# Seven block products in place of eight for the values of stage two of an attention layer

## The chip, the cores and the metric

The kernel runs on one core of a Trainium2 chip. The core has TensorE for matmuls (it accumulates into eight banks of PSUM, 128 partitions of 512 float32 each), VectorE, ScalarE and GpSimd for the rest, and SyncE (SP), whose queue issues most of the transfers between DRAM and SBUF. The program gives each engine its instructions in the order in which it emits them; semaphores order the engines among each other. The metric is device time in microseconds (us) for one execution; lower is better.

## The reference

One layer: RMS norm, one input projection into q, k, v and a gate (1024 to 4096 columns), neighbourhood attention over a grid of 32 x 64 tokens with 16 heads of 64, gate, output projection, residual, final RMS norm. Sequence 2048, model width 1024, float32.

```python
def rmsnorm(x, g):
    xf = x.astype(jnp.float32)
    y = xf * lax.rsqrt(jnp.mean(xf * xf, axis=-1, keepdims=True) + RMS_EPS)
    return (y * g.astype(jnp.float32)).astype(x.dtype)

def neighbourhood_mixer(h, w_in, rpb):
    B, S, _ = h.shape
    proj = h @ w_in
    q, k, v, gate = jnp.split(proj, 4, axis=-1)
    heads = lambda a: a.reshape(B, S, N_HEADS, HEAD_DIM)
    o = neighbourhood_attention(heads(q), heads(k), heads(v), rpb)
    return o.reshape(B, S, D_INNER), gate

...
        h = rmsnorm(x, g)
...
            o, gate = neighbourhood_mixer(h, w_in, rpb)
...
        x = x + (o * jax.nn.silu(gate)) @ w_out
    return rmsnorm(x, norm_f)
```

The change concerns `v`, for the second half of the tokens.

## The kernel before

**Precision.** Every float32 matrix is split into a high part h (rounded by a ScalarE copy into float32r) and a low part l = x - h (a VectorE subtraction). A product is three matmuls: h h, h l and l h. One split is therefore one ScalarE and one VectorE operation on a tile of 128 x 512.

**Stages.** Tokens are worked in two halves of 1024, each as two chunks of 512 columns. Stage one (`stage_one`) takes chunks 0 and 1: first the values (two groups u of four head pairs, 512 columns each, token tiles t = 0 to 7 of 128), then twelve *units* of q, k and gate columns. Stage two (`stage_two`) takes chunks 2 and 3: values for token tiles 8 to 15, then nine units. After that the rest of the projections is mixed with attention, and at last comes the output projection.

**Seven products.** The q, k and gate units already use seven block products in place of eight (`seven_products`). The normalised x of a half is cut into blocks Bij (model rows i, chunk j), the weights into Aij (A12: output block 1, model rows 2). `order7` and `uses` say which sum meets which:

```python
order7 = (1, 6, 2, 7, 5, 4, 3)
uses = {1: ("A11", "B11"), 2: ("A12", "B21"), 3: ("S4", "B22"), 4: ("A22", "T4"),
        5: ("S1", "T1"), 6: ("S2", "T2"), 7: ("S3", "T3")}
```

S1 = A21 + A22, S2 = S1 - A11, S3 = A11 - A21 and S4 = A12 - S2 are sums of weights; T1 to T4 are sums of x blocks in the same manner. A product is 12 matmuls of 128 x 128 by 128 x 512 (4 blocks of 128 model rows, 3 matmuls each). P1 gets a bank; a copy of it (`keep`) is kept in SBUF, and P2 adds into the same bank, which then is finished. P6 gets a bank; VectorE writes the bank plus the copy of P1 to u ("2"), then P7 adds into the bank, u ("3") is made, then P4 adds. P5 gets a third bank, and P3 adds into it. So a product that adds into a bank waits for the VectorE or ScalarE operation that reads the bank before it. `run` emits, after each product, what reads its bank, then what is left of the product before (`give`: scale or gate, and a store to DRAM a few matmuls later), then `ahead` (weight loads for unit n + 2, sums for unit n + 1, splits of weights six products ahead), then `also`, with hooks by unit m and product i. In stage one the outputs of chunks 0 and 1 are multiplied by the inverse norm after the product, three of four on GpSimd (line 458); in stage two x is normalised before.

**Values before the change.** In stage two the values are the plain sum over eight blocks: `pair` and `values_of` (line 562) take each of 16 (u, t) tiles with 8 x 3 matmuls, u = 0 in pairs of token tiles, u = 1 mostly one tile at a time. Weights come in raw (`load_v0`) and are split (`split_v`, lines 542 and 545); weights of u = 0 are loaded and, for three of four blocks, split during the last unit of stage one. `evac_v` (line 394) copies a finished bank to SBUF with ScalarE, and a store to `vd` follows. Between the tiles stand, written out by hand, the normalisation of chunk 3 (`normed`, line 516, which needs the spread inverse norm of `spread_rstd(3)`), the splits of x (lines 520 and 521), the sums T (lines 908 to 916) and the first weights of the units (`ahead`).

**Buffers.** `wp` holds eight slots for split weights, `raw` six for raw weights, `xs` 32 for split x blocks, `ev` eight for outputs on their way to DRAM; a pool's slot is reused once all readers of its last tile are done. `store(key, lag, f)` issues f some matmuls later in the order of emission; `due` counts matmuls.

Of the kernel before, what the change touches and what calls it, by code (L numbers as in the profile page):

```python
# [10 lines left out]
F32 = mybir.dt.float32  # L11
# [60 lines left out]
def build(ctx, tc, x, xr, xt, wg, rpb, last, w_out, n0, nf, masks, out):  # L72
    nc = tc.nc
# [4 lines left out]
    sgd = [dram.tile([128, S], F32, name=f"sgd{p}") for p in range(NP)]  # L78
    vd = [dram.tile([4, S, 128], F32, name=f"vd{u}") for u in range(2)]
    ogd = [dram.tile([128, 4, NP, 128], F32, name=f"ogd{T}") for T in range(4)]  # L80
    wod = {f: dram.tile([128, 4, 2, 512], F32, name=f"wod{f}") for f in ("T1", "T2", "T3", "T4")}

    def pool(name, bufs):
# [431 lines left out]
    def normed(f, c, k, t):  # L515
        nc.vector.scalar_tensor_tensor(t, t, gain(f, k), rb[c], op0=OP.mult, op1=OP.mult)
# [56 lines left out]
    def stage_one():  # L573
# [30 lines left out]
            for t, j in hs:  # L604
                square(t, j, rows_in.pop((t, j)))

        def also(n, i):
            m = n + len(us) - 1
            if (m, i) == (4, 0):
                reorder_rstd(0)  # L610
                reorder_rstd(1)
# [189 lines left out]
    def stage_two():  # L801
# [3 lines left out]
        for k in range(4):  # L805
            load_x(2, "x22", k, x22[k])
        slots = {"T2": [(mp, 512)] * 8,
                 "T3": [(sp, 512)] * 2 + sixth[:5] + [(lp, 512)],
                 "T4": [(vh, 512)] * 4 + [(mp, 512)] * 2 + [sixth[5], (qp, 512)]}

        OW = {}

# [61 lines left out]

        ahead, run = seven_products(units_two, 2, X2, also)

        def pair(u, ts, *do):
            for b in range(4):
                values_of(X2, u, ts, (2 * b, 2 * b + 1))
                if b < len(do):  # L880
                    do[b]()

        def both(*fs):
            return lambda: [f() for f in fs]

        def block(f, x, *ks):
            def g():
                if f not in X2:
                    X2[f] = [(xs([128, 512], F32R, "h"), xs([128, 512], F32R, "l")) for _ in range(4)]
                for k in ks:  # L890
                    normed(f, 3, k, x[k])
                    split_to(*X2[f][k], x[k], None)
            return g

        def w(u, b):
            return lambda: [split_v(u, a, b) for a in range(2)]

        def lw(u, *bs):
            return lambda: [load_v0(u, a, b) for b in bs for a in range(2)]

        def v(u, *ts):
            return lambda: [evac_v(u, t, ps[t]) for t in ts]

        def t123(*ks):
            def g():
                for k in ks:
                    a, b, c = x11[k], x12[k], x22[k]
                    nc.vector.tensor_tensor(c, c, b, OP.subtract)
                    nc.vector.tensor_tensor(b, b, a, OP.subtract)
                    nc.vector.tensor_tensor(a, a, c, OP.add)  # L910
            return g

        def t4(*ks):
            def g():
                for k in ks:
                    nc.vector.tensor_tensor(x21[k], x21[k], x11[k], OP.subtract)
            return g

        def form(f, x, *ks):
            def g():  # L920
                for k in ks:
                    h, l = (place_of(a) for a in slots[f][2 * k:2 * k + 2])
                    X2.setdefault(f, []).append((h, l))
                    split_to(h, l, x[k], None)
            return g

        def t1(*ks):
            def g():
                for k in ks:
                    split_to(*X2["B12"][k], x12[k], None)  # L930
                X2["T1"] = X2["B12"]
            return g
# [800 lines left out]
```

## Time and profile before

| | us |
|---|---|
| median of 3 runs | 1047.72 |
| lowest, highest | 1047.21, 1049.62 |
| the profiled execution, device time | 1047.92 |
| its span, first to last instruction | 1046.1 |
| stage one's values end, its units begin | 95.4 |
| stage two's values | 325.3 to 412.9 |
| stage two's units begin | 412.9 |

In the profile PE is TensorE's matmuls, PEld its weight loads, DVE VectorE, ACT ScalarE, POOL GpSimd, SPq the queue of SP. A row of a group reads: line, engine, operation, out<-in by the program's names, shape, count | busy us, mean ns of one | idle time of the engine before them, and what ended it. A timeline row reads: start, length, engine, line, operation, count, and in brackets the idle time before it. Records of matmuls overlap, as the array is pipelined.

### The profile page before, as it was taken

Reading aid. Unit: us, or ns where it says so; the run is one execution under the profiler, and the core shown is the slowest. Engines: PE = TensorE matmul, PEld = TensorE weight load, DVE = VectorE, ACT = ScalarE, POOL = GpSimd, SP = SyncE. Lnnn points to the kernel's source line nnn. Section 1 sums busy time; section 2 is a strip of 40 time slices with the busy share of each in tenths; the row PEclk is TensorE's granted clock in tenths of the full one; section 3 lists DMA queues with packets and bytes.
Section 4 is the critical chain, followed back from the end, with each engine's and each line's share of the span. In section 5 each row is a group of like instructions: output and inputs, shape, how many; then the busy total and the mean of one; then the engine's idle time right before and its main releaser. Section 6 shows DMA issues by size and latency. Waiting matters only on the chain.

```text
span 1046.1 us, 20290 instructions
## 1 busy us (share of the span) xinstructions
PE 1035.6 (99%) x7256; PEld 848.4 (81%) x7256; DVE 736.4 (70%) x1606; ACT 558.0 (53%) x1305; POOL 263.0 (25%) x352
## 2 busy tenths in 40 slices
PE   9999999999999999999999999999999999999997
PEld 6888888887888888888888788888888787888876
DVE  5375657778897724766765775667777788777876
ACT  7545323344344334333434477787888877664433
POOL 0000231221221000000000476765556432420000
PEclk9999999999999999999999999999999999999999
DMA  8733544442736424556565777878777599899553
GB/s 300 243 101 101 141 142 132 131 148 94 211 97 197 121 81 106 206 174 218 179 206 191 231 243 216 251 212 280 252 236 247 182 276 311 270 339 382 134 167 101
DMA packets 133213, 205.30 MB, mean 196 GB/s; under 512 B 12216, under 2 KB 56504, under 8 KB 133112
## 3 DMA queue, kind: packets, MB, share of 16 engines
q1 hardware_dynamic: 131240, 200.99, 61.1%
q0 software_dynamic: 1440, 2.62, 1.7%
q8 instruction: 57, 0.93, 0.4%
q10 hardware_dynamic: 432, 0.40, 0.1%
q14 instruction: 44, 0.36, 0.1%
HBM read 145.24 MB, written 58.72 MB: 195 GB/s over the span
## 4 chain that ended last, share of the span: by engine, by line
PE 95%; DVE 2%; DMA 1%; ACT 1%; issue 0%; SPq 0%; ACTq 0%; DVEq 0%
PE pp L438 37%; PE pv L562 17%; PE py L1463 9%; PE s L1073 8%; PE o L1180 8%; PE ph L1158 4%; PE pp L384 2%; PE pp L386 2%; PE pp L382 2%; PE po L1381 2%; PE po L1383 2%; PE po L1385 2%; DMA sgt<-sgd 1%; DVE f L421 0%; DMA vt<-vd 0%
## 5 line engine op out<-in xcount | busy, mean ns | idle before, releaser
L438 PE MATMUL pp<-h,f 128*128 128x512 f32 x672 | 217.4, 389 | 0.0
L1087 ACT ACTIVATE x<-x,st 128x360 f32<-128x360 f32 (+5 forms) x256 | 151.2, 593 | 24.8 <-DVE st L1081 24.8
L438 PEld LDWEIGHTS pp<-h,f 128*128 128x128 f32 x672 | 126.1, 188 | 26.2
L438 PE MATMUL pp<-t,f 128*128 128x512 f32 x558 | 141.7, 389 | 0.1
L1101 POOL TENSOR_SCALAR x<-x,st 128x480 f32<-128x480 f32 (+5 forms) x192 | 114.5, 614 | 94.3 <-DVE st L1092 92.0
L438 PE MATMUL pp<-l,f 128*128 128x512 f32 x336 | 130.7, 389 | 0.0
L458 POOL TENSOR_TENSOR tmp<-tmp,rb 128x512 f32<-128x512 f32 x36 | 58.4, 1622 | 270.4 <-DVE tmp L456 233.6
L1081 DVE CUSTOM_DVE_ANT_0 x<-s,em 128x360 f32<-128x360 f32 (+5 forms) x256 | 123.0, 535 | 0.6 <-PE s L1073 0.5
L438 PEld LDWEIGHTS pp<-t,f 128*128 128x128 f32 x558 | 104.7, 188 | 22.3 <-DVE u L451 0.6
L1041 POOL TENSOR_TENSOR em<-e,mk 128x264 f32<-128x264 f32 (+3 forms) x64 | 50.8, 824 | 259.5 <-DMA mk<-in_masks_dram 246.0
L421 DVE TENSOR_TENSOR f<-raw,f 128x512 fp32r<-128x512 f32 x105 | 76.5, 728 | 41.8 <-ACT f L420 41.8
L1073 PE MATMUL s<-kt,q 64*128 64x480 f32 (+5 forms) x512 | 95.3, 487 | 0.1
L1180 PEld LDWEIGHTS o<-pta,vt 120*64 120x64 f32 (+2 forms) x1792 | 80.9, 137 | 14.4 <-DVE st L1081 13.6
L562 PE MATMUL pv<-wh,h 128*128 128x512 f32 x256 | 89.1, 394 | 0.7 <-ACT wh L542 0.7
L562 PE MATMUL pv<-wl,h 128*128 128x512 f32 x256 | 88.6, 391 | 0.0
L562 PE MATMUL pv<-wh,l 128*128 128x512 f32 x256 | 88.6, 391 | 0.0
L1180 PE MATMUL o<-pta,vt 120*64 120x128 f32 (+5 forms) x1792 | 85.5, 253 | 0.5 <-DVE pta L1134 0.4
L1073 PEld LDWEIGHTS s<-kt,q 64*128 64x128 f32 x512 | 64.7, 186 | 16.3 <-DVE pta L1134 2.1
L420 ACT ACTIVATE f<-raw 128x512 fp32r<-128x512 f32 x105 | 63.5, 623 | 20.0 <-PE pp L438 8.3
L438 PEld LDWEIGHTS pp<-l,f 128*128 128x128 f32 x336 | 63.1, 188 | 13.1
L1134 DVE COPY pta<-ph 120x512 f32<-120x512 f32 (+5 forms) x96 | 56.9, 639 | 23.7 <-PE ph L1158 23.5
L1134 ACT ACTIVATE pta<-ph 120x512 f32<-120x512 f32 (+5 forms) x96 | 49.7, 557 | 37.0 <-PE ph L1158 36.2
(187 smaller groups left out, 1836.3 us busy)
## 6 DMA issues: line engine op xcount, KB each, us to landing
raw<-in_wg_dram SPq DMA_DIRECT2D x124, 256.0 KB, 4.3
row<-in_xr_dram SPq DMA_DIRECT2D x32, 256.0 KB, 4.8
vd<-v SPq DMA_DIRECT2D x32, 256.0 KB, 2.6
sgd<-sg SPq DMA_DIRECT2D x32, 256.0 KB, 2.9
q<-qd SPq DMA_DIRECT2D x32, 256.0 KB, 5.5
sgt<-sgd SPq DMA_DIRECT2D x32, 256.0 KB, 5.7
ogd<-og SPq DMA_DIRECT2D x32, 256.0 KB, 3.5
kt<-kd SPq DMA_DIRECT2D x16, 480.0 KB, 6.5
```

The source lines that it names most:

```text
L420: nc.scalar.activation(t[:, 0], src, AF.Copy)
L421: nc.vector.tensor_tensor(t[:, 1], src, t[:, 0].bitcast(F32), OP.subtract)
L438: nc.tensor.matmul(B[n, P], t[:, int(m == 2), c], x[k][int(m == 1)], start=P in (1, 6, 5) and k == 0 and m == 0, stop=k == 3 and m == 2, s ...
L458: nc.gpsimd.tensor_tensor(tmp, tmp, rb[c], OP.mult)
L562: nc.tensor.matmul(ps[t], a[:, o], b, start=k == 0 and m == 0, stop=k == NK - 1 and m == 2)
L1073: nc.tensor.matmul(pst[s], qt[a, qs], kt[a, :r1 - r0, c0:c1].rearrange("p r (s c) -> p s r c", c=8), start=True, stop=True)
L1081: nc.vector.tensor_tensor_reduce(X[i, C][s], pst[s], EM[p, ROW_TYPE[T], COL_TYPE[C], s], -1.0, 1e38, OP.add, OP.min, st[:, o:o + 1])
L1087: nc.scalar.activation(X[i, C][s], X[i, C][s], AF.Exp, bias=st[:, o:o + 1], scale=-1.0, accum_out=st[:, 4 + o:5 + o])
L1101: nc.gpsimd.tensor_scalar(X[i, C][s], X[i, C][s], st[:, o:o + 1], 1.0, op0=OP.mult, op1=OP.mult)
L1134: (nc.vector.tensor_copy if h else lambda o, i_: nc.scalar.activation(o, i_, AF.Copy))(t[:k, h, b * 512:b * 512 + w], banks_[b, h][:k, :w])
L1180: nc.tensor.matmul(to.rearrange("d (h q) -> d h q", q=64) if nq > 64 else to, vt[:k, strip, s * 64:s * 64 + 64], t[:k, h, at:at + 64] if n ...
L1463: nc.tensor.matmul(B[m, P], t[:, a, c], b, start=P in (1, 6, 5) and k == 0 and i == 0, stop=k == 3 and i == 2, skip_group_check=True)
```

## The change

Stage two's values become seven products as well. The blocks are the same; now the weights are the moving operand: Aij are blocks of the value weights (A11 and A12: u = 0 with model rows 1 and 2; A21 and A22: u = 1), and each product has four tiles of 128 tokens. A product's tile i is 12 matmuls of one `values_product(P, i)`; the order is P1, P2, P6, P7, P5, P4, P3, four tiles each. U1 (ScalarE, half of P1), U2 and U3 (VectorE) take the places of the copies above. P2's tiles go out through ScalarE as before, the outputs of P5, P4 and P3 through VectorE (`give_v`), which adds U as it scales by 0.5.

The sums S1 to S4 of the value weights are made during stage one's units 0 to 7: in units 0, 2, 4 and 6 (one quarter j of the weights each) four loads at product 0 (`value_rows`) and four VectorE sums at products 3 to 6 (`value_sum`); S1 and S4 are stored raw to `vsd`. In units 1, 3, 5 and 7 S3 and S2 are split (`value_split`, products 1 and 3) and their halves are stored to `vsp`. In stage two `load_s` brings split S2 and S3 straight into `wp` slots, and S1, S4 and A22 raw, to be split by `split_s`. `plan` gives, for each tile, what is emitted behind it. The raw weights of u = 1 are no longer loaded there, except A22. `spread_rstd(3)` moves ahead of the first product; the sums T2 and T3 now go to tiles of their own, so x11 and x22 keep their values for T1, T4 and B22; T1 gets its own tiles instead of overwriting the split B12, which is no longer made. The first `ahead` calls for the units come six to nine tiles (of 12 matmuls) before the end instead of eight to nine tiles of 24. T3 and T4 exchange one slot (`lp`, `qp`).

```diff
@@ -78,6 +78,8 @@
+    vsd = {f: dram.tile([4, 128, 512], F32, name=f"vsd{f}") for f in ("S1", "S4")}
+    vsp = {f: dram.tile([4, 2, 128, 512], F32, name=f"vsp{f}") for f in ("S2", "S3")}
@@ -604,8 +606,40 @@
+        VS = {}
+        def value_rows(j):
+            spot = mkp([128, 3, 512], F32, "vs")
+            homes = [spot[:, k] for k in range(3)] + [kp([128, 960], F32, "vs")[:, :512]]
+            a, b = j % 2, j // 2
+            for f, u, h in (("A21", 1, 0), ("A22", 1, 2), ("A11", 0, 0), ("A12", 0, 2)):
+                VS[f] = homes.pop()
+                o = 512 * (b + h)
+                nc.sync.dma_start(VS[f], wg[KINDS["v"] + 2 * u + a, :, o:o + 512])
+        def value_sum(j, f):
+            a, b, to, o = {"S1": ("A21", "A22", "A22", OP.add), "S3": ("A11", "A21", "A21", OP.subtract),
+                           "S2": ("S1", "A11", "A11", OP.subtract), "S4": ("A12", "S2", "A12", OP.subtract)}[f]
+            nc.vector.tensor_tensor(VS[to], VS[a], VS[b], o)
+            VS[f] = s = VS[to]
+            if f in vsd:
+                store(("vs", f, j), 3, lambda: nc.sync.dma_start(vsd[f][j], s))
+        def value_split(j, f):
+            h, l = ev([128, 512], F32R, "vsh"), ev([128, 512], F32R, "vsl")
+            split_to(h, l, VS[f], None)
+            for i, s in enumerate((h, l)):
+                store(("vs", f, j, i), 5, lambda i=i, s=s: nc.sync.dma_start(vsp[f][j, i], s.bitcast(F32)))
         def also(n, i):
             m = n + len(us) - 1
+            if m < 8:
+                if m % 2 == 0 and i == 0:
+                    value_rows(m // 2)
+                if m % 2 == 0 and i in (3, 4, 5, 6):
+                    value_sum(m // 2, ("S1", "S3", "S2", "S4")[i - 3])
+                if m % 2 == 1 and i in (1, 3):
+                    value_split(m // 2, "S3" if i == 1 else "S2")
@@ -805,8 +839,8 @@
-                 "T3": [(sp, 512)] * 2 + sixth[:5] + [(lp, 512)],
-                 "T4": [(vh, 512)] * 4 + [(mp, 512)] * 2 + [sixth[5], (qp, 512)]}
+                 "T3": [(sp, 512)] * 2 + sixth[:5] + [(qp, 512)],
+                 "T4": [(vh, 512)] * 4 + [(mp, 512)] * 2 + [sixth[5], (lp, 512)]}
@@ -874,77 +908,143 @@
...
-        def w(u, b):
-            return lambda: [split_v(u, a, b) for a in range(2)]
-        def lw(u, *bs):
-            return lambda: [load_v0(u, a, b) for b in bs for a in range(2)]
-        def v(u, *ts):
-            return lambda: [evac_v(u, t, ps[t]) for t in ts]
...
+        U1, U2, U3, B = {}, {}, {}, {}
+        w_of = {1: ((0, 0), (0, 1)), 2: ((0, 2), (0, 3)), 3: (("S4", 0), ("S4", 1)), 4: (("A22", 0), ("A22", 1)),
+                5: (("S1", 0), ("S1", 1)), 6: (("S2", 0), ("S2", 1)), 7: (("S3", 0), ("S3", 1))}
+        def load_s(q, *js):
+            for j in js:
+                if q in vsp:
+                    a, b = j % 2, j // 2
+                    if a == 0:
+                        W[q, b] = wp([128, 2, 512], F32R, "wh"), wp([128, 2, 512], F32R, "wl")
+                    for i, t in enumerate(W[q, b]):
+                        nc.sync.dma_start(t[:, :, a * 256:a * 256 + 256].bitcast(F32), vsp[q][j, i].rearrange("p (k c) -> p k c", c=256))
+                    continue
+                VR[q, j] = t = raw([128, 512], F32, "raw")
+                nc.sync.dma_start(t, wg[KINDS["v"] + 2 + j % 2, :, 1024 + 512 * (j // 2):1536 + 512 * (j // 2)] if q == "A22" else vsd[q][j])
+        def split_s(q, *js):
+            for j in js:
+                a, b = j % 2, j // 2
+                if a == 0:
+                    W[q, b] = wp([128, 2, 512], F32R, "wh"), wp([128, 2, 512], F32R, "wl")
+                h, l = (t[:, :, a * 256:a * 256 + 256] for t in W[q, b])
+                split_to(h, l, VR.pop((q, j)).rearrange("p (k c) -> p k c", c=256), None)
+        def half(to, ps, u):
+            nc.vector.scalar_tensor_tensor(to, ps, 0.5, u, op0=OP.mult, op1=OP.add)
+        def give_v(u, t, ps, add):
+            v = ev([128, 512], F32, "v")
+            half(v, ps, add)
+            dst = vd[u].rearrange("h n d -> n h d")[t * 128:t * 128 + 128]
+            written.add(("v", u, t))
+            store(("v", u, t), 8, lambda: nc.sync.dma_start(dst, v.rearrange("p (h d) -> p h d", h=4)))
+        def values_product(P, i):
+            if P in (1, 6, 5):
+                B[P, i] = bank(512, "pv")
+                for Q in {1: (2,), 6: (7, 4), 5: (3,)}[P]:
+                    B[Q, i] = B[P, i]
+            ps = B[P, i]
+            f = uses[P][1]
+            o = slice(i * 128, i * 128 + 128)
+            for k in range(4):
+                x, w = X2[f][k], [a[:, k % 2] for a in W[w_of[P][k // 2]]]
+                for m, (a, b) in enumerate(((x[0], w[0]), (x[0], w[1]), (x[1], w[0]))):
+                    nc.tensor.matmul(ps, a[:, o], b, start=P in (1, 6, 5) and k == 0 and m == 0, stop=k == 3 and m == 2,
+                                     skip_group_check=True)
+                    due(1)
+            if P == 1:
+                U1[i] = ep([128, 512], F32, "u1") if i < 2 else kp([128, 960], F32, "u1")[:, :512]
+                nc.scalar.activation(U1[i], ps, AF.Copy, scale=0.5)
+            elif P == 2:
+                evac_v(0, 8 + i, ps)
+            elif P == 6:
+                U2[i] = ev([128, 512], F32, "u2")
+                half(U2[i], ps, U1[i])
+            elif P == 7:
+                U3[i] = xp([128, 512], F32, "u3")
+                half(U3[i], ps, U1[i])
+            elif P == 5:
+                give_v(1, 12 + i, ps, U3[i])
+            elif P == 4:
+                give_v(1, 8 + i, ps, U1[i])
+            else:
+                give_v(0, 12 + i, ps, U2[i])
+        T3, T2 = {}, {}
+        def norm(f, x, *ks):
+            for k in ks:
+                normed(f, 3, k, x[k])
+        def sum3(*ks):
+            for k in ks:
+                T3[k] = xs([128, 512], F32, "t3")
+                nc.vector.tensor_tensor(T3[k], x22[k], x12[k], OP.subtract)
+        def sum2(*ks):
+            for k in ks:
+                T2[k] = xs([128, 512], F32, "t2")
+                nc.vector.tensor_tensor(T2[k], x11[k], T3[k], OP.add)
+        def sum1(*ks):
+            for k in ks:
+                nc.vector.tensor_tensor(x12[k], x12[k], x11[k], OP.subtract)
+        def sum4(*ks):
+            for k in ks:
+                nc.vector.tensor_tensor(x21[k], x21[k], T2[k], OP.subtract)
         def form(f, x, *ks):
-            def g():
-                for k in ks:
+            for k in ks:
+                if f in slots:
                     h, l = (place_of(a) for a in slots[f][2 * k:2 * k + 2])
-                    X2.setdefault(f, []).append((h, l))
-                    split_to(h, l, x[k], None)
-            return g
-        def t1(*ks):
-            def g():
-                for k in ks:
-                    split_to(*X2["B12"][k], x12[k], None)
-                X2["T1"] = X2["B12"]
-            return g
-        pair(0, (8, 9), both(w(0, 3), lambda: spread_rstd(3)), both(lw(1, 0), block("B12", x12, 0, 1)), block("B12", x12, 2, 3),
-             block("B22", x22, 0, 1))
-        pair(0, (10, 11), both(v(0, 8, 9), block("B22", x22, 2, 3)), t123(0), t123(1), lw(1, 1))
-        pair(0, (12, 13), v(0, 10, 11), t123(2), t123(3), both(t4(0, 1, 2, 3), lw(1, 2)))
-        pair(0, (14, 15), both(v(0, 12, 13), w(1, 0)), both(w(1, 1), lw(1, 3)), w(1, 2), w(1, 3))
-        pair(1, (12,), v(0, 14, 15), form("T2", x11, 0), form("T2", x11, 1))
-        pair(1, (13,), both(v(1, 12), form("T2", x11, 2)), form("T2", x11, 3))
-        pair(1, (14,), both(v(1, 13), form("T3", x22, 0)), form("T3", x22, 1))
-        pair(1, (15,), both(v(1, 14), lambda: ahead(-9, -1)), form("T3", x22, 2), form("T3", x22, 3))
-        pair(1, (8,), both(v(1, 15), lambda: ahead(-8, -1)), t1(0), t1(1), lambda: ahead(-7, -1))
-        pair(1, (9,), both(v(1, 8), t1(2)), t1(3), lambda: ahead(-6, -1), form("T4", x21, 0))
-        pair(1, (10,), both(v(1, 9), form("T4", x21, 1)), form("T4", x21, 2), form("T4", x21, 3))
-        pair(1, (11,), both(v(1, 10), lambda: ahead(-5)), lambda: ahead(-4), both(lambda: ahead(-3), lambda: ahead(-2)),
-             both(lambda: ahead(-1), v(1, 11)))
+                else:
+                    h, l = xs([128, 512], F32R, "h"), xs([128, 512], F32R, "l")
+                X2.setdefault(f, []).append((h, l))
+                split_to(h, l, x[k], None)
+        all4 = (0, 1, 2, 3)
+        plan = {
+            (1, 0): [(split_v, 0, 0, 3), (split_v, 0, 1, 3)],
+            (1, 1): [(norm, "x12", x12, *all4)],
+            (1, 2): [(norm, "x22", x22, *all4)],
+            (1, 3): [(sum3, *all4), (load_s, "S2", 0, 1)],
+            (2, 0): [(sum2, *all4), (load_s, "S2", 2, 3)],
+            (2, 1): [(form, "T2", T2, 0, 1)],
+            (2, 2): [(form, "T2", T2, 2, 3)],
+            (2, 3): [(form, "B22", x22, *all4), (load_s, "S3", 0, 1)],
+            (6, 0): [(form, "T3", T3, 0, 1), (load_s, "S3", 2, 3)],
+            (6, 1): [(form, "T3", T3, 2, 3), (load_s, "S1", *all4)],
+            (6, 2): [(sum4, *all4)],
+            (6, 3): [(sum1, *all4)],
+            (7, 0): [(form, "T1", x12, 0, 1)],
+            (7, 1): [(split_s, "S1", 0, 1)],
+            (7, 2): [(split_s, "S1", 2, 3), (form, "T1", x12, 2, 3)],
+            (7, 3): [(load_s, "A22", *all4)],
+            (5, 0): [(form, "T4", x21, 0)],
+            (5, 1): [(form, "T4", x21, 1), (split_s, "A22", 0, 1)],
+            (5, 2): [(form, "T4", x21, 2), (split_s, "A22", 2, 3), (load_s, "S4", *all4)],
+            (5, 3): [(form, "T4", x21, 3)],
+            (4, 0): [(split_s, "S4", 0, 1)],
+            (4, 1): [(split_s, "S4", 2, 3), (ahead, -9, -1), (ahead, -8, -1)],
+            (4, 2): [(ahead, -7, -1)],
+            (4, 3): [(ahead, -6, -1)],
+            (3, 0): [(ahead, -5)],
+            (3, 1): [(ahead, -4)],
+            (3, 2): [(ahead, -3)],
+            (3, 3): [(ahead, -2), (ahead, -1)],
+        }
+        spread_rstd(3)
+        for P in (1, 2, 6, 7, 5, 4, 3):
+            for i in range(4):
+                values_product(P, i)
+                for f, *a in plan[P, i]:
+                    f(*a)
+        X2["B12"] = X2["T1"]
```

More of the change, by code (lines that the diff above doesn't have):

```diff
@@ L875, in stage_two @@
         ahead, run = seven_products(units_two, 2, X2, also)
[L877 to L886, printed above, removed]
-            def g():
-                if f not in X2:
-                    X2[f] = [(xs([128, 512], F32R, "h"), xs([128, 512], F32R, "l")) for _ in range(4)]
-                for k in ks:
-                    normed(f, 3, k, x[k])
-                    split_to(*X2[f][k], x[k], None)
-            return g
@@ L895, in w @@
-        def w(u, b):
-            return lambda: [split_v(u, a, b) for a in range(2)]
-        def lw(u, *bs):
-            return lambda: [load_v0(u, a, b) for b in bs for a in range(2)]
-        def v(u, *ts):
-            return lambda: [evac_v(u, t, ps[t]) for t in ts]
-        def t123(*ks):
-            def g():
-                for k in ks:
[L907 to L910, printed above, removed]
-            return g
@@ L913, in t4 @@
[L913 to L917, printed above, removed]
+        U1, U2, U3, B = {}, {}, {}, {}
[12 more added lines that the diff above has]
+                nc.sync.dma_start(t, wg[KINDS["v"] + 2 + j % 2, :, 1024 + 512 * (j // 2):1536 + 512 * (j // 2)] if q == "A22" else vsd[q][j])
@@ L919, in form @@
+        def sum4(*ks):
+            for k in ks:
+                nc.vector.tensor_tensor(x21[k], x21[k], T2[k], OP.subtract)
         def form(f, x, *ks):
-            def g():
-                for k in ks:
+            for k in ks:
+                if f in slots:
                     h, l = (place_of(a) for a in slots[f][2 * k:2 * k + 2])
-                    X2.setdefault(f, []).append((h, l))
-                    split_to(h, l, x[k], None)
-            return g
-        def t1(*ks):
-            def g():
-                for k in ks:
-                    split_to(*X2["B12"][k], x12[k], None)
-                X2["T1"] = X2["B12"]
-            return g
```

## The prediction

> **What bounds the kernel now.** I read the page first: span, busy times, clock row, chain that ended last.
>
> ```profile
> span 1046.1 us, 20290 instructions
> PE 1035.6 (99%) x7256; PEld 848.4 (81%) x7256; DVE 736.4 (70%) x1606; ACT 558.0 (53%) x1305; POOL 263.0 (25%) x352
> PEclk9999999999999999999999999999999999999999
> PE 95%; DVE 2%; DMA 1%; ACT 1%; issue 0%; SPq 0%; ACTq 0%; DVEq 0%
> ```
>
> TensorE sets the end: 95% of the chain, clock at full speed in every slice. But "busy" doesn't tell what one matmul costs, since their records overlap. So I read the chain in order of time (start, length, what), and the group of stage two's value matmuls in the window 326 to 412.
>
> ```profile
> 95.61 146.89 PE pp L438 x648
> ...
> 325.45 2.73 PE pv L562 x12
> 328.66 84.37 PE pv L562 x372
> 413.03 171.36 PE pp L438 x756
> L562 PE MATMUL pv<-wh,l 128*128 128x512 f32 x127 | 44.2, 389 | 0.0
> ```
>
> One record lasts 389 ns, but 372 matmuls take 84.37 us: 226.8 ns each. That pace is the price of a matmul; stage one's seven-product loop has the same (146.89 / 648 = 226.7). Stage two's values are 12 + 372 = 384 matmuls, 87.1 us, with no idle time before them.
>
> **The change, part by part.**
>
> *Removed matmuls.* Before: 16 tiles x 8 contraction blocks x 3 = 384. After: 7 products x 4 tiles x 4 blocks x 3 = 336. 48 go, at 226.8 ns: **-10.89 us**. All of them lie on the chain. The new ones go twelve in a row into one bank instead of alternating between two; the x648 row is such a loop, so I price that at 0. A tile takes 12 x 0.2268 = 2.72 us. Nothing else is to be gained in this stage, because TensorE has no idle time in it.
>
> *What comes in its place must stay hidden.* Three stretches: the eight units of stage one that get new work, its last four units, and stage two.
>
> ```profile
> core 0: us, PE busy (x) PEld busy (x) DVE busy (x) ACT busy (x) POOL busy (x), PEclk, DMA share, GB/s
> 95.40:248.00 152.60, 152.60 (x675) 126.33 (x675) 106.11 (x156) 55.40 (x110) 37.49 (x23) 1.00 0.46 138
> ...
> 248.00:325.30 77.30, 77.04 (x339) 63.09 (x338) 68.81 (x110) 35.10 (x64) 19.16 (x12) 1.00 0.49 152
> 325.30:412.90 87.60, 87.60 (x388) 72.48 (x387) 46.68 (x73) 32.24 (x58) 1.71 (x2) 1.00 0.39 109
> ```
>
> *Stage two, VectorE and ScalarE.* VectorE had 58 large operations of its own here (10 weight splits, 8 normalisations, 8 + 16 splits of x, 16 sums). Now 78: 2 weight splits, 8 normalisations, 16 sums, 20 splits of x, 12 splits of weight sums, 20 additions out of PSUM. 20 more at 0.69 us (rows below) are 13.8 us: 46.7 becomes some 60 of 76.7 us. ScalarE goes from 50 to 42 operations. Neither is full, so what counts is when each result is wanted. The tightest is T2 for P6, the third product, since spread, normalisation and two sums of four blocks come before it.
>
> ```profile
> 330.80 0.69 DVE L363 SCALAR_TENSOR_TENSOR sg<-sg,tmp 128x512 f32<-128x512 f32 x1 [1.85 <-ACT sg L362]
> ...
> 332.61 0.74 DVE L516 SCALAR_TENSOR_TENSOR land<-land,g,rb 128x512 f32<-128x512 f32 x1
> ...
> 349.03 0.68 DVE L908 TENSOR_TENSOR land<-land 128x512 f32<-128x512 f32 x1
> ```
>
> The queue of SP, and the landing times of such loads between 300 and 345:
>
> ```profile
> 324.64 4.06 SPq L513 DMA_DIRECT2D land<-in_xt_dram  x4
> DMA to landing us min/median/max: 3.9/5.2/5.8
> ```
>
> Stage one's tail (the row at 330.80) holds VectorE until 331.4, and that stays. TensorE passes the two spread matmuls and starts P1 at about 325.8; P6 starts eight tiles later, at 347.5. VectorE: two weight splits, now behind two more ScalarE copies (rb and U1), to 333.9; eight normalisations at 0.74 to 339.8; eight sums at 0.68 to 345.3; then T2's four low halves, the last at about 348.1. P6 reads them at 347.9, 348.6, 349.3 and 350, so the margin is 1 to 2 us; whole durations (0.68 and 0.74) are counted, and operations that follow one another overlap a little. The x22 loads issued until 328.7 land before 334.5 and are wanted at 336.9. Cost taken: **0**; ends: 0, and 2 us if the tail is later by as much.
>
> *Stage two, weights.* S2 and S3 come split from DRAM, as eight transfers of 256 KB each, straight into the slots that P1 and P2 free. SP stands before the first until P1's last tile, four tiles (10.9 us) ahead of P6. Behind SP's wait only the stores of values are queued, and nobody waits for these in this stage.
>
> ```profile
> raw<-in_wg_dram SPq DMA_DIRECT2D x124, 256.0 KB, 4.3
> DMA packets 3029, 5.54 MB, mean 231 GB/s; under 512 B 337, under 2 KB 337, under 8 KB 3027
> GB/s 225 328 372 365 335 358 321 113 44 150 222 239 307 270 191 143 181 283 389 396 239 137 393 89 72 126 147 249 335 335 249 242 201 154 389 174 68 143 106 143
> ```
>
> The last two rows are the DMA view of 312 to 336, with eighteen 256 KB transfers. The slots of P1's first two blocks are free at 335.3, so SP starts there; alone, a transfer lands in 4.3 us, and the seven behind it (1.84 MB) take 4.6 us at the best rate, 396 GB/s, and 7.9 at the mean. S2 is complete between 344.2 and 347.5; its second half is wanted at 348.9. Two value stores in between, at the mean rate 2.3 us, would make it 0.9 us late. Pieces of 1 KB are read here, and no row shows such reads in bulk. S3 has the same time from P2's last tile to P7. Cost: 0 to 1.8 us for both; I take **0**, because only the slowest case with the stores in the way is late. S1, A22 and S4 are asked for three or more tiles (8 us) before P5, P4 and P3 need them, and the rows of unit zero three tiles before their first form: 0.
>
> *Stage one, units 0 to 7.* In each even unit 4 loads, 4 VectorE sums and 2 stores; in each odd unit 2 splits (a ScalarE copy and a VectorE subtraction) and 4 stores. 24 VectorE operations at 0.69 us make 106.1 of 152.6 us 122.7. 40 transfers of 256 KB (10.5 MB) add 69 GB/s to 138. What matters is that P7 adds into P6's bank, so its first matmul waits for VectorE's addition u of P6, due one product (2.72 us) after P6's end. Unit 4 into unit 5: VectorE, then GpSimd, TensorE and SP's queue.
>
> ```profile
> 185.46 0.69 DVE L456 TENSOR_TENSOR tmp<-pp,u 128x512 f32<-128x512 f32 x1 [1.49 <-PE pp L438]
> ...
> 186.67 1.78 DVE L427 TENSOR_TENSOR raw<-raw,s 128x512 f32<-128x512 f32 x1
> ...
> 189.13 0.69 DVE L421 TENSOR_TENSOR f<-s,f 128x512 fp32r<-128x512 f32 x1
> 190.90 0.69 DVE L456 TENSOR_TENSOR tmp<-pp,u 128x512 f32<-128x512 f32 x1 [1.08 <-PE pp L438]
> ...
> 195.84 0.68 DVE L427 TENSOR_TENSOR s<-raw 128x512 f32<-128x512 f32 x1
> 196.44 0.68 DVE L451 TENSOR_TENSOR u<-pp,p 128x512 f32<-128x512 f32 x1
> 186.29 1.62 POOL L458 TENSOR_TENSOR tmp<-tmp,rb 128x512 f32<-128x512 f32 x1 [11.98 <-DMA raw<-in_wg_dram]
> 189.14 1.83 POOL L458 TENSOR_TENSOR tmp<-tmp,rb 128x512 f32<-128x512 f32 x1 [1.23 <-DVE tmp L456]
> 198.81 0.84 PE L438 MATMUL pp<-t,f 128*128 128x512 f32 x3
> 172.21 0.38 SPq L415 DMA_DIRECT2D raw<-in_wg_dram  x1
> ...
> 181.73 1.40 SPq L415 DMA_DIRECT2D raw<-in_wg_dram  x3
> ```
>
> S1 falls into the idle 1.49 us before 185.46. S3 falls behind the 1.78 us sum and pushes the next addition by 0.6. S2 comes at about 189.7, while GpSimd multiplies: the sum at 186.67, two SBUF inputs, lasted until GpSimd's operation was over (1.78 for 0.69), so I let S2 take 1.78 too, ready at 191.5 to 192. S4 the same, at 195.4. Then u, at 196.44 before, starts at about 197.1 and ends at 197.8; P7 starts at 198.81. Margin 1.0 us, cost **0**. The Trainium skill (GPSIMD Engine Reference, section Specifications) says that GpSimd's SBUF interfaces are shared with VectorE and contended for by instructions with two SBUF inputs; 1.78 for 0.69 agrees. By that rule the new sums are of the kind that suffers, which the second rival prices. One more sum held up, at 1.09 us, would eat the margin; two would stall 1.2 us, in four even units 4.8 us. The other end is 0. In odd units only two subtractions come, two products apart, and their copies find ScalarE busy 55.4 of 152.6 us. SP now stands before the S1 store until VectorE is done, some 184.6; behind it are the next weight rows (at 181.73 before), which land by 190.5 and are first added at 195.84.
>
> *Sum.* Profiled execution 1047.92 (span 1046.1, and 1.8 around it) - 10.89 = 1037.0. Against the median of the runs, 1047.72, it is 0.20 high: 1036.8. I add 0.2 for a short wait of the size that the middle row of windows shows (77.30 - 77.04 = 0.26): **1037.0**.
>
> **Rivals.** Chances stand with them.
>
> 1. *Forecast (0.70):* all new work hidden, 1036.0 to 1038.3.
> 2. *GpSimd holds up more value sums than I let it (0.12):* P7 waits for u in the even units. For: 1.78 us rows. Against: in units 8 to 11 VectorE is already busier (68.8 of 77.3 us) and TensorE lost 0.26 us. 1.2 to 4.8 us: 1038.2 to 1041.8, middle 1040.
> 3. *P6 and P7 wait for their weights, or P6 for T2 (0.10):* 1.2 to 3.8 us (the upper ends above, 1.8 and 2), 1038.2 to 1040.8. For: margins of 1 to 2 us. Against: only the slow end of each bound is late.
> 4. *Slower (0.04):* the rows of the value sums land late, so S1 blocks VectorE in front of P5's addition. They are asked for at the unit's first product, behind a store on which SP may stand; S1 runs four products in. In unit 4, SP would issue them from 172.6, behind the row at 172.21, to 174.4, and S1 wants them at 183.9, after the work that ends 1.49 us before 185.46. To lose 10.9 us in four even units each must lose 2.7, so they would have to land about 5 us after that, 15 us after issue; from there each microsecond more costs four. Landing at 190: some 3.7 us each, 14.8: 1051.8. Against: landings of 4.3 us.
> 5. *Nothing gained (0.04):* not by a wrong count, since the 48 matmuls do go, but by rivals 2 and 3 at their upper ends and more: 1046 to 1049.
>
> **How the numbers follow.** A measurement here tells no change from 0.2%, 2.1 us: 1045.6 to 1049.8. Faster: cases 1 to 3 and a part of 5, 0.93. Same: 0.03. Slower: 0.04. The range starts 1 us under the forecast, as stage three's small waits can shift, and goes to 1041, which takes in most of rivals 2 and 3.
>
> **What would show it.** Right: 336 value matmuls in stage two at 227 ns, some 76.4 us from first to last; the loop of units after it starts near 402 instead of 413; u in stage one a microsecond later at most, no new wait of TensorE over 0.5 us. Wrong: waits at pv for wh or wl (SP's transfers) or for T2; waits at pp for u in units 1, 3, 5 and 7; value sums of 1.78 us in a row. If the gap from the loop to the end changes by over 1 us, the gain or loss lies outside what I worked out.

## The result and the profile after

| | before | after |
|---|---|---|
| median of 4 runs, us | 1047.47 | 1035.70 |
| lowest to highest | 1047.01 to 1049.62 | 1035.47 to 1039.73 |
| ratio of the two | | 0.9893, 95% interval 0.9865 to 0.992 |
| profiled execution: device time, span | 1047.92, 1046.1 | 1035.70, 1033.9 |

The forecast was 1037.0, with a range that by the prediction's text starts 1 us under it and goes to 1041. The median of these runs lies just under that low end, 0.3 us under 1036.0; a second set of runs of the same kernel (e5 below) had 1036.62. From the 1047.72 that the prediction started with, 10.7 us were forecast to go; here 11.8 went, there 9.6.

The page of the profile after, the same rows as before:

```profile
span 1033.9 us, 20333 instructions
PE 1022.7 (99%) x7208; PEld 838.6 (81%) x7208; DVE 768.7 (74%) x1650; ACT 557.5 (54%) x1305; POOL 263.6 (25%) x352
PEclk9999999999999999999999999999999999999998
PE 95%; DVE 3%; ACT 1%; issue 1%; DMA 0%; SPq 0%; DVEq 0%; ACTq 0%
```

TensorE still ends the chain. It issues 48 matmuls fewer (7256 to 7208); VectorE has 32 us more work. Its share of the chain is 3% where it was 2%, but none of the new sums (L623) stands in the chain. The chain in order of time (start, length, what) and the waits of TensorE over the whole execution:

```profile
93.44 146.89 PE pp L440 x648
...
257.94 65.31 PE pp L440 x288
323.73 76.21 PE pv L956 x336
399.93 171.36 PE pp L440 x756
PE py L1563 <- ACT f L1534: 1.3, 1, 1.3
PE zp L128 <- DVE z L125: 1.2, 1, 1.2
PE o L1280 <- DVE pta L1234: 0.4, 1, 0.4
```

The 336 value matmuls take 76.21 us, 226.8 ns each: the pace is the same as that of the 372 before. No wait over 0.15 us stands at the value matmuls (pv) or at the units (pp). Cutting both executions where the first matmul of each stage starts shows where the time went:

| stretch, us | before | after | difference |
|---|---|---|---|
| start to stage one's first unit | 95.44 | 93.28 | -2.16 |
| stage one's twelve units | 229.85 | 229.80 | -0.05 |
| stage two's values, with the spread | 87.58 | 76.69 | -10.89 |
| from there to the end of the last matmul | 627.08 | 626.50 | -0.58 |
| last matmul to the end of the span | 6.20 | 7.65 | +1.45 |
| span | 1046.1 | 1033.9 | -12.2 |

Stage two lost 10.89 us, the number of the forecast. The first and the last two lines lie where the program is unchanged; e5 below asks whether they belong to the change.

The same three stretches as before by their place in the program, 2.2 us earlier:

```profile
core 0: us, PE busy (x) PEld busy (x) DVE busy (x) ACT busy (x) POOL busy (x), PEclk, DMA share, GB/s
93.20:245.80 152.60, 152.60 (x675) 126.36 (x674) 127.17 (x180) 59.46 (x118) 38.08 (x23) 1.00 0.67 205
245.80:323.10 77.30, 77.03 (x339) 63.11 (x338) 68.85 (x110) 34.81 (x64) 19.23 (x12) 1.00 0.51 156
323.10:400.70 77.60, 77.60 (x344) 64.20 (x343) 58.37 (x94) 28.21 (x51) 1.69 (x2) 1.00 0.60 184
```

VectorE now has 127 of 152.6 us in the eight units, and 58 of 77.6 in stage two; memory traffic went from 138 to 205 GB/s and from 109 to 184. TensorE is without a gap in both. Unit 4 into unit 5 in VectorE's queue, then GpSimd's, SP's and TensorE's:

```profile
180.52 0.69 DVE L453 TENSOR_TENSOR u<-pp,p 128x512 f32<-128x512 f32 x1 [0.83 <-PE pp L440]
181.13 0.68 DVE L423 TENSOR_TENSOR f<-raw,f 128x512 fp32r<-128x512 f32 x1
181.72 0.69 DVE L623 TENSOR_TENSOR vs<-vs 128x512 f32<-128x512 f32 x1
...
184.45 1.78 DVE L429 TENSOR_TENSOR raw<-raw,s 128x512 f32<-128x512 f32 x1
186.15 0.68 DVE L623 TENSOR_TENSOR vs<-vs 128x512 f32<-128x512 f32 x1
...
187.95 1.78 DVE L623 TENSOR_TENSOR vs<-vs 128x512 f32<-128x512 f32 x1
...
191.00 1.79 DVE L623 TENSOR_TENSOR vs<-vs 128x512 f32<-128x512 f32 x1
...
194.67 0.68 DVE L453 TENSOR_TENSOR u<-pp,p 128x512 f32<-128x512 f32 x1
184.06 1.61 POOL L460 TENSOR_TENSOR tmp<-tmp,rb 128x512 f32<-128x512 f32 x1 [11.93 <-DVE tmp L458]
187.51 1.67 POOL L460 TENSOR_TENSOR tmp<-tmp,rb 128x512 f32<-128x512 f32 x1 [1.84 <-DVE tmp L458]
190.40 1.84 POOL L460 TENSOR_TENSOR tmp<-tmp,rb 128x512 f32<-128x512 f32 x1 [1.23 <-DVE tmp L458]
182.44 0.33 SPq L626 DMA_DIRECT2D vsdS<-vs  x1
...
183.29 1.42 SPq L417 DMA_DIRECT2D raw<-in_wg_dram  x3
196.64 0.84 PE L440 MATMUL pp<-t,f 128*128 128x512 f32 x3
```

The four value sums (L623): the first in VectorE's idle time, the second behind the long sum at 184.45, the third and fourth held up to 1.78 and 1.79 us by GpSimd. The long sum and these two each begin while a GpSimd operation runs, and end 0.55 us after it. The addition u ends at 195.35 and P7 starts at 196.64: 1.3 us to spare. Stage two's tight places, T2's low halves and S2's transfers:

```profile
341.41 1.29 DVE L523 TENSOR_TENSOR t<-t,t 128x512 fp32r<-128x512 f32 x2
344.00 1.29 DVE L523 TENSOR_TENSOR t<-t,t 128x512 fp32r<-128x512 f32 x2 [1.31 <-ACT t L522]
333.10 0.64 SPq L922 DMA_DIRECT2D wh<-vspS  x1
...
337.71 0.60 SPq L922 DMA_DIRECT2D wl<-vspS  x1
DMA to landing us min/median/max: 3.8/5.3/5.5
```

P6 starts at 345.3 here and reads the last half of T2, ready at 345.3, some 2.5 us later. S2's last transfer is issued by 338.3 and has landed by 343.8 at the latest (low halves land in 3.8 to 5.5 us); its second half is wanted at 346.7. The value stores come behind S2's transfers here, from 338.4, so the case with the stores in between did not occur.

### The profile page after: what moved, and what is told of

Same layout as the page of the kernel before. It is cut to its first block, busy times and chain, and to the rows that moved or that the text cites. A ratio compares the mean times of both kernels' runs of the same rounds, so it can differ in the third digit from the quotient of the medians.

```text
span 1033.9 us, 20333 instructions
## 1 busy us (share of the span) xinstructions
PE 1022.7 (99%) x7208; PEld 838.6 (81%) x7208; DVE 768.7 (74%) x1650; ACT 557.5 (54%) x1305; POOL 263.6 (25%) x352
## 4 chain that ended last, share of the span: by engine, by line
PE 95%; DVE 3%; ACT 1%; issue 1%; DMA 0%; SPq 0%; DVEq 0%; ACTq 0%
PE pp L440 37%; PE py L1563 9%; PE pv L564 8%; PE s L1173 8%; PE o L1280 8%; PE pv L956 7%; PE ph L1258 4%; PE pp L386 2%; PE po L1481 2%; PE pp L388 2%; PE pp L384 2%; PE po L1483 2%; PE po L1485 2%; DVE f L423 1%; DVE x L1181 0%
## 5 line engine op out<-in xcount | busy, mean ns | idle before, releaser
L423 DVE TENSOR_TENSOR f<-raw,f 128x512 fp32r<-128x512 f32 x105 | 75.2, 716 | 28.9 <-ACT f L422 28.5
L422 ACT ACTIVATE f<-s 128x512 fp32r<-128x512 f32 x42 | 26.3, 625 | 53.2 <-DVE s L429 49.5
L440 PE MATMUL pp<-sixths,f 128*128 128x512 f32 x198 | 54.6, 389 | 0.0
L1258 PEld LDWEIGHTS ph<-ident,x 64*120 64x120 f32 (+2 forms) x1408 | 42.5, 128 | 11.3 <-issue 8.5
```

What stands on the lines that cost most here:

```text
L422: nc.scalar.activation(t[:, 0], src, AF.Copy)
L423: nc.vector.tensor_tensor(t[:, 1], src, t[:, 0].bitcast(F32), OP.subtract)
L440: nc.tensor.matmul(B[n, P], t[:, int(m == 2), c], x[k][int(m == 1)], start=P in (1, 6, 5) and k == 0 and m == 0, stop=k == 3 and m == 2, s ...
L1258: nc.tensor.transpose(banks_[o // 512, h][:k, o % 512:o % 512 + 64], X[2 * m + b, C][s][q, at:at + k], ident[q, q])
```

## The experiments

All times of a set are from one chip, with the kernel before run beside them: 1046.29 us in the median (29 executions) for e1 to e4, 1046.19 (15) for e5 to e8.

**e1, stage one's additions alone.** The kernel before with the new work of units 0 to 7, its stage two left as it was.

```diff
         def also(n, i):
             m = n + len(us) - 1
+            if m < 8:
+                if m % 2 == 0 and i == 0:
+                    value_rows(m // 2)
+                if m % 2 == 0 and i in (3, 4, 5, 6):
+                    value_sum(m // 2, ("S1", "S3", "S2", "S4")[i - 3])
+                if m % 2 == 1 and i in (1, 3):
+                    value_split(m // 2, "S3" if i == 1 else "S2")
```

> The kernel before, with the change's additions to stage one alone (16 loads, 16 sums, 8 splits, 24 stores in units 0 to 7; nobody reads what they store). Theory (48 matmuls fewer, all else hidden): the additions cost nothing, 1047.5 us, within 0.5 of the kernel before; stage one's units still take 229.8 us. Rival (GpSimd holds up the sums and P7 waits for VectorE): 1.2 to 4.8 us slower, 1048.7 to 1052.3, with waits of TensorE in units 1, 3, 5 and 7.

1045.66 us (11 executions), ratio 0.9996 with an interval of 0.9988 to 1.0005. The median is 0.6 us under the kernel before, a little more than the 0.5 that I allowed, but the interval takes in no change. Stage one's units take 229.80 us:

```profile
95.95 146.89 PE pp L440 x648
...
260.45 65.31 PE pp L440 x288
```

These are the stretches of the kernel before (146.89 and 65.34 us), and no wait of TensorE there is over 0.15 us. The additions cost nothing that can be seen; the rival, 1.2 us or more, falls.

**e2, P1 twice.** The 48 matmuls put back, all else as changed.

```diff
-            for k in range(4):
+            for k in (0, 1, 2, 3) * (2 if P == 1 else 1):
```

> The changed kernel with P1's 48 matmuls in stage two issued twice (the second time over the same bank, so the output stays). Theory: the gain is the 48 matmuls at 226.8 ns, so it goes back by 10.9 us, to 1046.6 with the changed kernel at 1035.7; stage two takes 87.6 us again. Rival (part of the gain of 11.8 us in the medians comes from something else that the change relieves, SP's queue or memory): what returns is 10.9 all the same, but the time then stays 0.9 us or more under the kernel before, 1046.6 or less against 1047.5, in stretches outside stage two; by the theory these differ only as single executions do.

1046.05 us (12 executions), ratio to the kernel before 0.9997, interval 0.9987 to 1.0006. In the chain of this kernel:

```profile
324.39 87.09 PE pv L956 x384
```

384 matmuls, 87.09 us, as in the kernel before, and stage two takes 87.57 us with its spread. With their number equal the two kernels are equally fast, so the gain is the 48 matmuls and nothing else that can be seen. The rival's 0.9 us is not excluded by these times alone: the median is 0.24 us under the kernel before, and the interval reaches 1.4 under it.

**e3, the value sums three times.** This takes the margin of u away.

```diff
+            for acc in accs[:2]:
+                nc.vector.tensor_tensor(acc, VS[a], VS[b], o)
             nc.vector.tensor_tensor(VS[to], VS[a], VS[b], o)
```

> The changed kernel with each value sum of stage one made three times (twice into spare tiles): 8 more VectorE operations of 0.69 us with two SBUF inputs in each of units 0, 2, 4 and 6. In the changed kernel's trace the addition u of unit 5 ends 1.3 us before P7 needs it. Theory (the margin is about 1 us and then TensorE stalls): 8 x 0.61 = 4.9 us less the idle time of some 1.5 us, so u comes 1 to 3 us too late in each of the four odd units: 4 to 12 us slower, 1040 to 1048, with TensorE's waits for u before P7 in units 1, 3, 5 and 7. Rival (the buffers between the engines let VectorE run later without harm): within 1 us of 1035.7.

1048.75 us (10 executions), slower than the kernel before by a ratio of 1.0022 (1.001 to 1.0035), and 12 to 13 us slower than the changed kernel's medians in the other sets: at and past the upper end of what I expected. Stage one takes 241.08 us, 11.28 more. Waits of TensorE in the window of stage one, then its matmuls behind the third wait:

```profile
PE pp L440 <- DVE u L453: 8.4, 5, 2.1
```

```profile
204.43 1.55 PE L440 MATMUL pp<-t,f 128*128 128x512 f32 x3 [2.01 <-DVE u L453]
205.78 1.48 PE L440 MATMUL pp<-sixths,f 128*128 128x512 f32 x3
207.06 1.98 PE L440 MATMUL pp<-t,f 128*128 128x512 f32 x6
208.87 0.39 PE L440 MATMUL pp<-h,f 128*128 128x512 f32 x1
```

The place is the one foreseen: P7 waits for u, in units 1, 3, 5 and 7, with 2.0 to 2.1 us each (the fifth wait, 0.26, is in unit 8; it is 0.15 in the changed kernel). Four waits are 8.2 us; counted from start to start, less the pace of 0.227, they cost 8.8. Most of the rest is the pace after the third: the twelve matmuls from 204.43 to 208.87 take 4.44 us in place of 2.72. In the stretch 204.4 to 208.5 the granted clock is 0.58:

```profile
204.40:208.50 4.10, 4.07 (x11) 3.21 (x12) 3.58 (x6) 1.26 (x2) 0.00 (x0) 0.58 1.00 229
```

The last 0.8 us are small delays at the other restarts and in unit 8. The profiled execution, 1046.59 us, is nearly the fastest of the ten (1046.52 to 1052.29). The mean granted clock on record is 0.996 to 0.998 in the four fastest and 0.993 and 0.994 in the two slowest, so the slow ones probably had more such stretches; no trace of them shows it.

**e4, S2 asked for three tiles later.**

```diff
-            (1, 3): [(sum3, *all4), (load_s, "S2", 0, 1)],
-            (2, 0): [(sum2, *all4), (load_s, "S2", 2, 3)],
+            (1, 3): [(sum3, *all4)],
+            (2, 0): [(sum2, *all4)],
...
-            (2, 2): [(form, "T2", T2, 2, 3)],
+            (2, 2): [(form, "T2", T2, 2, 3), (load_s, "S2", 0, 1, 2, 3)],
```

> The changed kernel with the eight loads of S2 asked for three tiles of matmuls later, behind the third tile of P2. In the changed kernel's trace they are issued from 333.1 to 338.3 and P6 starts at 345.3. Theory: SP first waits for the value copy at about 340.5, issues from 341 to 346, so the first half lands near 348 and the second near 351; P6 starts 2.5 to 3.5 us late and waits once more for 1 to 2 us: 3.5 to 5 us slower, 1039.2 to 1040.7. Rival (weights are covered by some slack I don't see): no change, 1035.7. A third outcome: the wait costs more than its own length, because TensorE's clock falls; then matmuls after it show a pace over 227 ns.

1042.05 us (4 executions), some 5.4 us over e5's median and 6.4 over the first median of the changed kernel. Stage two takes 81.55 us in place of 76.69: 4.86 more. SP issues the first of the eight at 341.61 and the last by 346.8, as worked out. TensorE's matmuls at P6's start, and the windows around them:

```profile
346.71 0.47 PE L956 MATMUL pv<-wh,t 128*128 128x512 f32 x1 [0.79 <-DMA wh<-vspS]
349.29 0.77 PE L956 MATMUL pv<-wl,t 128*128 128x512 f32 x1 [2.12 <-DMA wl<-vspS]
349.86 1.05 PE L956 MATMUL pv<-wh,t 128*128 128x512 f32 x2
350.71 0.63 PE L956 MATMUL pv<-wl,t 128*128 128x512 f32 x1
```

```profile
349.30:352.30 3.00, 3.00 (x7) 2.05 (x8) 0.30 (x1) 1.41 (x3) 0.00 (x0) 0.53 1.06 352
352.40:356.00 3.60, 3.60 (x17) 2.95 (x16) 1.89 (x3) 0.00 (x0) 0.00 (x0) 1.00 1.10 374
```

Waits of 2.9 us, within what the first half's landing was expected to cost, then seven matmuls from 349.29 to 352.37, 3.08 us in place of 1.59, at a granted clock of 0.53. The second wait that I expected, for S2's second half, is not there: the first wait and the slow pace gave it the time. So in this execution, the fastest of the four (1040.69), stage two's total came out right and its second part was another; the third outcome is what happened. The median lies 1.3 us over the upper end that I expected.

**e5, the changed kernel again.**

> The changed kernel once more, many executions beside the kernel before. Theory: the difference of medians is the 10.9 us of the 48 matmuls, within 0.6; the 11.8 us of the first comparison, and the 12.2 us of the two profiled spans, hold 1 us or more that belongs to single executions (the start 2.2 us shorter, the end after the last matmul 1.5 us longer). Rival: the change itself makes start or end other, and the difference stays at 11.8.

1036.62 us (1036.02 to 1037.26, 4 executions) against 1046.19: 9.6 us, ratio 0.9907 (0.9893 to 0.992). The first comparison had 11.8. The theory's 10.9 lies between and in the intervals of both, though neither set came within the 0.6 us that I allowed. In its profiled execution the stretches of the table above are 93.97, 229.81, 76.69, 628.36 and 6.55 us. Stages one and two agree to 0.01 us with the first profile of this kernel; the start is 0.7 longer, the part behind stage two 1.9 longer, and the end after the last matmul 1.1 shorter. So these three move by 0.7 to 1.9 us between executions of one kernel, and the 1.3 us that the two first spans differ by beyond 10.89 need no other cause.

**e6, the value sums twice.** As e3, with one copy.

> The changed kernel with each value sum of stage one made twice (once into a spare tile): 4 more VectorE operations in each even unit. With three sums P7 waited 2.2 us in each odd unit, and without copies u ends 1.3 us early: 8 operations pushed it by 3.5 us, so 4 push it by 1.7, and P7 waits some 0.4 us four times: 1 to 2 us slower than the changed kernel if TensorE's clock holds, up to 6 if it falls to half for 3 us after such a wait. Rival (the margin was larger than the trace of one unit shows): no wait, same time.

1036.99 us (1036.67 to 1037.42, 4 executions), 0.4 over e5 with overlapping executions: less than expected. Stage one takes 230.64 us, 0.8 more, with no wait that the trace lists in units 1, 3, 5 and 7. VectorE in unit 4, copy (L624) and sum (L625), and u, then GpSimd:

```profile
189.61 1.77 DVE L624 TENSOR_TENSOR acc<-vs 128x512 f32<-128x512 f32 x1
191.42 0.69 DVE L625 TENSOR_TENSOR vs<-vs 128x512 f32<-128x512 f32 x1
...
193.23 1.78 DVE L624 TENSOR_TENSOR acc<-vs 128x512 f32<-128x512 f32 x1
195.04 0.69 DVE L625 TENSOR_TENSOR vs<-vs 128x512 f32<-128x512 f32 x1
...
196.88 0.68 DVE L453 TENSOR_TENSOR u<-pp,p 128x512 f32<-128x512 f32 x1
189.17 1.67 POOL L460 TENSOR_TENSOR tmp<-tmp,rb 128x512 f32<-128x512 f32 x1 [2.56 <-DVE tmp L458]
192.79 1.67 POOL L460 TENSOR_TENSOR tmp<-tmp,rb 128x512 f32<-128x512 f32 x1 [1.95 <-DVE tmp L458]
```

Of two operations in a row only the one that meets GpSimd's is held up; the next takes 0.69. So a further sum costs 0.6 us and not 1.8, u ends at 197.56, and P7 starts at 197.62, just behind it. The margin is used up. Most of the 0.8 us is there: in each of the four odd units P7's first two matmuls start 0.27 and 0.34 us after the one before in place of 0.23, 0.15 us more, and unit 8's wait is 0.25 in place of 0.15.

**e7 and e8, ten warm-up matmuls,** in the changed kernel and in the kernel before.

```diff
-    for _ in range(8):
+    for _ in range(10):
         nc.tensor.matmul(zp, z[:, :128], z, start=True, stop=True)
```

> The changed kernel with ten matmuls before the first real one in place of eight. In the kernel before's profiled run TensorE idled 0.7 us before its first real matmul and then ran at half pace (0.43 us each) for 3 us, so its start took 2.2 us longer than in the changed kernel's, where there was no idle time. Theory: two more matmuls cover the arrival of the first weights, so every execution has the short start, or one up to 0.8 us longer: the median 0 to 1 us under the changed kernel, and the spread of executions smaller. Rival: the clock doesn't depend on that gap, and the median is 0.4 to 0.8 us higher by the matmuls added.

> The kernel before with ten matmuls before the first real one in place of eight. Theory: 0 to 2 us faster than the kernel before, by as much as its executions had the long start; the difference to the changed kernel with ten such matmuls is 10.9 us, within 0.5. Rival: as in the changed kernel, 0.4 to 0.8 us slower.

e7: 1035.75 us (4 executions), 0.9 under e5; ratio to the kernel before 0.9897 (0.9882 to 0.9912), which overlaps e5's interval. e8: 1046.77 (11 executions), ratio 1.0005 (0.9996 to 1.0014): not faster. In the two profiled executions the start takes 93.86 and 93.67 us, inside what eight matmuls give (93.28, 93.97 and, in the kernel before, 95.44). With eight matmuls six of the eight profiled executions have 93.3 to 94.1 too, and only before and e1 have 95.4 and 95.8, so two executions don't show that ten avoid the long start. Both kernels' spread stayed, and e8's profiled execution, with the short start, is the slowest of its eleven: the spread does not come from the start alone. In the kernel before ten matmuls are 0.6 us slower, the rival's figure; in the changed kernel they are 0.9 us faster, the theory's. Neither difference is clear of the intervals, and I don't claim a better version. The difference between e7 and e8 is 11.0 us; the theory said 10.9.

## Why the prediction was right

- **The price of a matmul.** The step that carried the forecast: 48 matmuls at the pace of the chain (226.8 ns), and not at the 389 ns that one record lasts. Stage two went from 87.58 to 76.69 us, 10.89; e2 returned it. By the records' length the gain would have been 18.7 us (48 x 389 ns).
- **Twelve matmuls into one bank, priced at 0.** Right: 336 in 76.21 us is the same pace.
- **Stage one hidden, margin 1.0 us.** Right in place and nearly in size: S2 and S4 took 1.78 and 1.79 us as assumed, u moved by 0.4 us (196.44 less the 2.17 us by which this execution is ahead is 194.27; it starts at 194.67) where I had 0.7, and 1.3 us are left. e1 shows the cost as 0, e6 and e3 where it would begin. The upper bound of the second rival was drawn wrongly in one respect: it priced every further sum at GpSimd's hold, and e6 shows that only the first of a row pays it. One reading was wrong too: the sum at 186.67 did not end with GpSimd's operation (186.29 + 1.62 = 187.91) but 0.54 us after it, at 188.45; its price, 1.78 us, was right. And the units that would wait for u are the odd ones, as the signs at the prediction's end have it, not the even ones of the rivals.
- **VectorE's load.** I put 24 new operations at 0.69 us and had 122.7 us for the eight units; it is 127.2, because eight of the sixteen sums are held up and last 1.78 us. This moved no time. In stage two 58.4 us were measured for my 60.
- **SP and the weight rows.** SP stores S1 at 182.44, where I had 184.6 less 2.2. The rows of the next weights follow at 183.29 and are first added after 194; the early loads of `value_rows` land 2.1 to 8.0 us after their issue, the last of unit 4 is issued by 172.5, and S1 starts at 181.72 without a wait, so the slower case had nothing to start from.
- **S2, S3 and T2.** T2 was ready 2.5 us before its last half is read, S2 some 3 us; I had 1 to 2, and 1.4 or more without the value stores in the way (0.9 late with them). My estimates were on the late side in both. e4 shows that the cover is real: three tiles (8.2 us) later cost 4.9 us.
- **The 0.2 us for a short wait** has no counterpart: the middle stretch shows 77.30 - 77.03 us, as before, so that wait was already in the time that I started from. The rest of the distance between 1037.0 and 1035.70, some 1.1 us, lies in the start and in the part behind stage two, where the program is unchanged and executions of one kernel differ by 1 to 2 us (e5). The size of the removed work was right to 0.01 us; how near the whole time comes to the forecast is chance to that extent, as the 11.8 and the 9.6 us of the two sets show.

## What to carry to other kernels

On a kernel bound by TensorE, price a removed matmul at the distance between starts in a long run of the chain, not at the length of its record; then the whole question is whether the new work has a place, and that is answered for each result by when it is wanted, not by the busy share. Work moved to an engine with 30% idle time was free up to a definite number of operations per unit (here four, with four more just at the edge and eight more costing more than the change had gained). A missed deadline can cost more than the wait: in e3 and e4 the granted clock was 0.58 and 0.53 for 3 to 4 us after some of the waits.

## What the hardware showed that I had not expected

**Half pace after a short wait.** In e4, after waits of 0.79 and 2.12 us with one matmul between them, TensorE ran at a granted clock of 0.53 for some 3 us; in e3 after one of four waits of 2.0 us, at 0.58 for 4 us; after the other three, of the same length, at 1.00 and full pace. The Trainium skill (TensorE: Matmul & The Clock Gate, section What's actually happening) describes a gate that halves the clock after an idle window of about 3.4 us and lifts that after a busy window as long, with windows that run freely. The halving (0.427 us from start to start in place of 0.227), its length and the chance in it agree with these rows; idle times of 2.0 us as such are shorter than that window, so the measurement puts the danger lower.

**VectorE behind GpSimd.** In units 0 to 7 of the changed kernel nineteen VectorE operations on 128 x 512 took 1.77 to 1.79 us. Each had two inputs in SBUF, began while a GpSimd operation was running and ended 0.55 us after it. One that had begun just before GpSimd's kept its 0.68 (187.35, L423), and one with an input in PSUM, wholly within a GpSimd operation, took 0.69 (later, at 267.05, L458).

**The start.** In the first profile of before TensorE idled 0.68 us ahead of its first real matmul and then needed 8 matmuls from 5.47 to 9.05 us, 0.45 each, though the granted clock is given as 1.00 there; with no idle time, in the changed kernel's profile, the half pace was over after two. Idle time at this place does not decide it alone: in e6's profile TensorE idled 1.04 us there and was at full pace after two matmuls, in e1's it idled 0.83 us and nine matmuls took 0.45 each. What makes the difference between executions is not settled.
